# TensorE's order in the expert stretch of a two-layer diffusion step pinned to the program's, with the four column-tiled products of a value step kept together

## The chip, the cores and the metric

The kernel runs on one core of a Trainium2 chip. The metric is the device time of one execution in microseconds, the median of several runs. The engines are named as in the profile: PE (TensorE, the matmuls), PEld (its weight loads), DVE (VectorE), ACT (ScalarE), POOL (GpSimd, which also issues the gathers here) and SP (SyncE, which issues the plain loads).

## The reference, cut to what matters

One inference step of a backbone of two layers. Each layer mixes tokens (attention, a recurrent cell, pooling) and then adds an expert block. There are 128 prompt tokens and 256 latent tokens. The change touches the expert block alone:

```python
def peer_ffn(x, w_q, sub_keys, u_table, v_table):
    q = (xt @ w_q).reshape(T, PEER_HEADS, 2, PEER_HALF)
    s = jnp.einsum('thcd,hckd->thck', q, sub_keys).astype(F32)
    top_s, top_i = lax.top_k(s, PEER_TOPK)
...
    expert = i1 * PEER_N_KEYS + i2
    gate = jax.nn.softmax(best_s, axis=-1).astype(x.dtype)
...
        a = jax.nn.gelu(jnp.einsum('thkd,td->thk', u_table[eb], xb), approximate=False)
        return jnp.einsum('thk,thkd->td', gb * a, v_table[eb])
```

Every token chooses 128 of 16384 experts (8 heads of 16); each expert has a row in `u_table` and one in `v_table`, both of 1024 numbers.

## The kernel before

The latent tokens and the prompt tokens take different ways through the expert block, and both run at once in what is called the dense stretch below (function `dense`, one per layer).

*Latent tokens, dense.* All 16384 experts are computed for all 256 tokens, and a table of gates G, nearly all zeros, weighs the result. 64 iterations (`bp`) take 256 experts each. `up` loads two blocks of `u` and multiplies them with the tokens' activations into a bank A; `weigh` multiplies the activated result by G and splits it into a high and a low half, W; `down` loads two blocks of `v` and adds the products into four banks `po`. Each 32-bit product is made by `mm3` in three passes from high and low halves (high by high, low of one, low of the other): 48 up-products and 24 down-products an iteration. ScalarE casts the high halves (L105) and VectorE subtracts for the low ones (L106). The first 23 iterations' up-products (`LOOK`) are made ahead, unsplit (`whole`, L1087), while routing and the gate table G are built; iterations 23 to 63 are made inside the dense stretch.

*Prompt tokens, gathered.* The generator `experts` goes through 128 steps of scores (rows of `u` gathered by POOL, tiles `gu`, dot products on VectorE, L883) and then, once the dots are transposed (`dT`, L877, and copied as `wT`), through 64 value steps in a layer (L896). Value step s takes the gathered tiles 2s and 2s+1 (`gv`), each brought by two gathers of 256 KB on POOL's queue (L869), issued three tiles ahead into five buffers. It makes four products, q = 0 to 3, each with 32 columns of weights `wz` and so in its own strip of 32 columns of the array; each shows as two records, so a step has eight. `wz` has one buffer, refilled before steps 0, 16, 32 and 48: POOL clears it (L889), VectorE makes four small copies from `wT` (L893). The clearing stands in POOL's queue behind the gathers of tile 2s+4.

*What sets the order.* `dense` writes, for each iteration, `up`, `weigh`, `down`, then as many steps of `experts` as are due by then: in the first half of a layer's value steps one or two an iteration, later mostly one. A scheduler that simulates the program may then move an engine's instructions against one another as far as data allow. `tc.keep_in_program_order` (here `behind`) forbids that for one instruction: it stays behind everything that was written before it for the same engine. Before, only the first of the four products of a value step was so pinned.

Of the kernel before, what the change touches and what calls it, by code (L numbers as in the profile page):

```python
# [22 lines left out]
KC = 8  # L23
# [45 lines left out]
def tile_hybrid_step(ctx: ExitStack, tc: tile.TileContext, I, O):  # L69
# [29 lines left out]
        return t  # L99


    PASSES = ((0, 0), (0, 1), (1, 0))

    def split_into(hi, lo, src):
# [24 lines left out]
        split_into(hi, lo, raw)  # L129
        return hi, lo  # L130

    def mm3(out, a, b, first, last):
        for n, (x, y) in enumerate(PASSES):
            pe.matmul(out, a[x], b[y], start=first and n == 0, stop=last and n == 2, skip_group_check=True)  # L134

    class Room:

# [13 lines left out]
            return t  # L151

    GATH = Room(stay, row=("gath", NGATH), half="half", quarter="half")


    behind = tc.keep_in_program_order


    ident = ld("ident", [P, P], I["c_ident"], cst)
# [19 lines left out]
    def tsl(i):  # L179
        return slice(i * P, (i + 1) * P)  # L180
# [592 lines left out]
    class Prompt:  # L773
# [65 lines left out]
        def experts(self):  # L839
# [7 lines left out]
            for k in range(2 * P + LAG):  # L847
# [33 lines left out]
                if 0 <= j < P:  # L881
                    u = late.pop(j)
                    behind(ve.scalar_tensor_tensor(u, u, 1.0, self.h2n, op0=ALU.mult, op1=ALU.mult, accum_out=dots[:, j:j + 1]))  # L883
                elif j >= P and (j - P) % 2 == 1:
                    r, h = (j - P) // 4, (j - P) // 2 % 2
                    if r % 8 == 0 and h == 0:

                        wz = stay.tile([P, 8, 4, 32], F32, tag="row", bufs=1, name=f"wz{l}{r}")
                        gp.memset(wz, 0.0)  # L889
                        flat = wz.rearrange("p r j c -> p (r j c)")  # L890
                        for q in range(4):
                            at = 32 * q + r
                            ve.tensor_copy(flat[:, at:at + 7 * 129 + 1:129], wT[:, at:at + 8])  # L893
                    v = [late.pop(j - 1), late.pop(j)]
                    for q in range(4):
                        m = pe.matmul(self.acc[h][32 * q:32 * q + 32, :], wz[:, r % 8, q, :],  # L896
                                      v[q // 2][:, q % 2 * 512:q % 2 * 512 + 512], start=(r == 0), stop=(r == 31),
                                      skip_group_check=True)
                        if q == 0:
                            behind(m)  # L900
                yield

    def queries(l, most):
# [111 lines left out]
    class Experts:  # L1015
# [56 lines left out]
        def up(self, whole=None):  # L1072

            l, bp = self.l, self.next
            if bp == NP:
                return
            self.next += 1

            pa = bank("pv" if bp % 2 and self.pr.done < P + LAG else "A", f"A{l}{bp}")
            for j in range(2):  # L1080
                u = (load_split if whole is None else load_whole)(I["u_T"][l, 2 * bp + j], f"u{l}{bp}{j}")
                out = pa[:, j * 256:(j + 1) * 256]
                for k in range(KC):
                    if whole is None:
                        mm3(out, [t[:, tsl(k)] for t in u], [t[:, k, :] for t in self.hs], k == 0, k == KC - 1)
                    else:
                        pe.matmul(out, u[:, tsl(k)], whole[:, k, :], start=k == 0, stop=k == KC - 1, skip_group_check=True)  # L1087
            gl = self.lay.tile([P, 2, 2 * P], F32, tag="gl", bufs=LOOK[l] - 1, name=f"gl{l}{bp}")
            ac.activation(gl, pa.rearrange("p (j t) -> p j t", j=2), AF.Gelu)  # L1089
            self.acts[bp] = gl  # L1090
# [11 lines left out]
        def down(self, po, bp, w):  # L1102
# [6 lines left out]
            for i, j in ((0, 0), (0, 1), (1, 0), (1, 1)) if end else ((0, 0), (1, 0), (0, 1), (1, 1)):  # L1109
                for h in range(2):  # L1110
                    mm3(po[i][h], [t[:, j, tsl(i)] for t in w], [t[:, h * 512:(h + 1) * 512] for t in v[j]],
                        bp == 0 and j == 0, end and j == 1)

    def dense(l, ex, p3, po, pr):

# [228 lines left out]
```

## Time and profile before

| | us |
|---|---|
| median of 3 runs | 2739.42 (2739.12 to 2743.07) |
| the profiled execution, own time | 2746.87 |
| its span, first to last instruction | 2745.1 |
| PE busy in it | 2500.7 (91%) |
| DVE, ACT, POOL busy | 1722.4, 1045.5, 927.6 |
| mean granted TensorE clock | 0.944 of full speed |

The table gives the whole span. The dense stretches are where the change lies; they run from about 683 to 1388 us and from about 2042 to 2732 us. In a timeline a row gives the start, the duration, the engine with line and operation, the tile written and those read, and how many instructions were merged; in brackets stands the engine's idle time just before and what ended it.

### The profile page before, as it was taken

To read this page: it belongs to the slowest core of one execution; us is meant where nothing else is said; L and a number is where in the kernel's file an instruction comes from. 1 tells how busy PE (TensorE), PEld (TensorE's weight loads), DVE (VectorE), ACT (ScalarE), POOL (GpSimd) and SP (SyncE) were. 2 spreads that over 40 slices of the span, in tenths; PEclk is the share of its full clock that TensorE was granted. 3 is DMA by queue.
4 is the path that set the end of the run, shared out by engine and by line. 5 is a ranking of instruction groups with operands and counts; after the bars stand their busy time and mean duration, and the time that the engine had idled before them with its cause. 6 is when DMAs were issued, how large, how long until landed. Compare 5 with 4: busy or idle time off the path is not lost.

```text
span 2745.1 us, 37514 instructions
## 1 busy us (share of the span) xinstructions
PE 2500.7 (91%) x13834; PEld 1915.5 (70%) x13834; DVE 1722.4 (63%) x3768; ACT 1045.5 (38%) x1545; POOL 927.6 (34%) x794
## 2 busy tenths in 40 slices
PE   7998779896999999999989885979969999999998
PEld 3744568785988777765666464868859877777665
DVE  4555979866877444443565468798778844444446
ACT  3434411544434433332444352114444433343333
POOL 0000034101445666754400002231224556656541
PEclk9998989897999999999999878999979999999999
DMA  7485589678899889897835644886999988888985
GB/s 258 139 269 194 167 289 337 210 268 321 305 352 347 303 314 330 290 330 259 292 122 166 218 162 152 315 291 232 334 347 353 329 296 311 299 315 289 330 294 192
DMA packets 217547, 749.33 MB, mean 273 GB/s; under 512 B 28308, under 2 KB 30868, under 8 KB 215316
## 3 DMA queue, kind: packets, MB, share of 16 engines
q1 hardware_dynamic: 137236, 444.91, 46.8%
q0 software_dynamic: 77824, 268.48, 27.9%
q10 hardware_dynamic: 2304, 33.56, 3.1%
q8 instruction: 108, 1.77, 0.3%
q14 instruction: 75, 0.61, 0.1%
HBM read 706.99 MB, written 39.85 MB: 272 GB/s over the span
## 4 chain that ended last, share of the span: by engine, by line
PE 62%; DMA 13%; DVE 12%; issue 7%; POOL 3%; ACT 2%; SPq 0%; POOLq 0%; DVEq 0%; ACTq 0%
PE po L134 22%; PE A L134 13%; PE pv L896 6%; DMA gu<-in_peer_u,ei 4%; PE A L1087 4%; PE pj_i L134 4%; DMA v_r<-in_peer_v 3%; DVE gu L883 3%; DMA gv<-in_v_half,eiT 2%; DMA wm<-in_w_mod 2%; PE pm L305 2%; POOL gu L863 2%; PE pj_t L134 2%; POOL gv L869 2%; PE pj_o L134 1%
## 5 line engine op out<-in xcount | busy, mean ns | idle before, releaser
L869 POOL DMA_INDIRECT gv<-in_v_half,eiT x512 | 590.1, 1153 | 437.7 <-PE pv L896 288.4
L134 PE MATMUL po<-v_h,W 128*128 128x512 f32 x2048 | 668.8, 398 | 30.5 <-ACT W L105 16.0
L863 POOL DMA_INDIRECT gu<-in_peer_u,ei x256 | 324.5, 1267 | 1095.0 <-DVE gu L883 474.6
L134 PEld LDWEIGHTS po<-v_h,W 128*128 128x128 f32 x2048 | 388.8, 191 | 160.7 <-ACT W L105 44.1
L106 DVE TENSOR_TENSOR v_l<-v_r,v_h 128x1024 fp32r<-128x1024 f32 x256 | 313.0, 1224 | 273.7 <-ACT v_h L105 273.5
L134 PE MATMUL A<-hs,u_h 128*128 128x256 f32 x2624 | 482.7, 284 | 1.3 <-ACT u_h L105 0.9
L134 PEld LDWEIGHTS A<-hs,u_h 128*128 128x128 f32 x2624 | 406.8, 189 | 58.9 <-issue 34.4
L105 ACT CAST v_h<-v_r 128x1024 fp32r<-128x1024 f32 x256 | 268.4, 1049 | 385.7 <-PE po L134 155.4
L134 PE MATMUL po<-v_l,W 128*128 128x512 f32 x1024 | 406.0, 397 | 0.1
L134 PE MATMUL A<-hs,u_l 128*128 128x256 f32 x1312 | 370.7, 283 | 2.4 <-DVE u_l L106 2.4
L106 DVE TENSOR_TENSOR u_l<-u_r,u_h 128x1024 fp32r<-128x1024 f32 x164 | 199.1, 1224 | 275.3 <-ACT u_h L105 275.2
L883 DVE SCALAR_TENSOR_TENSOR gu<-gu,h2n 128x1024 f32<-128x1024 f32 x256 | 307.4, 1218 | 63.7 <-DMA gu<-in_peer_u,ei 63.1
L1087 PE MATMUL A<-hw,u_r 128*128 128x256 f32 x1472 | 339.1, 386 | 0.0
L1087 PEld LDWEIGHTS A<-hw,u_r 128*128 128x128 f32 x1472 | 276.5, 193 | 36.0
L105 ACT CAST u_h<-u_r 128x1024 fp32r<-128x1024 f32 x164 | 171.4, 1050 | 307.8 <-PE A L134 258.5
L134 PEld LDWEIGHTS A<-hs,u_l 128*128 128x128 f32 x1312 | 248.3, 189 | 10.9 <-issue 6.7
L134 PEld LDWEIGHTS po<-v_l,W 128*128 128x128 f32 x1024 | 195.6, 191 | 49.6 <-issue 11.7
L896 PE MATMUL pv<-gv,wz 128*32 128x512 f32 x1024 | 194.2, 605 | 5.9 <-DVE wz L893 3.1
L106 DVE TENSOR_TENSOR W<-gl,W 128x512 fp32r<-128x512 f32 x128 | 87.9, 688 | 52.0 <-ACT W L105 51.9
L105 ACT CAST W<-gl 128x512 fp32r<-128x512 f32 x128 | 79.0, 618 | 105.7 <-PE po L134 72.0
L1089 ACT ACTIVATE gl<-A 128x512 f32<-128x512 f32 x128 | 75.5, 595 | 110.9 <-DVE W L106 62.9
L1046 PE MATMUL G<-o,o 128*128 128x128 f16 x1024 | 89.9, 238 | 30.0 <-DVE o L1038 27.6
(424 smaller groups left out, 2982.0 us busy)
## 6 DMA issues: line engine op xcount, KB each, us to landing
u_r<-in_u_T SPq DMA_DIRECT2D x256, 512.0 KB, 5.9
v_r<-in_peer_v SPq DMA_DIRECT2D x256, 512.0 KB, 5.1
wm<-in_w_mod SPq DMA_DIRECT2D x96, 512.0 KB, 5.7
gates<-stage ACTq DMA_DIRECT2D x14, 2048.0 KB, 10.9
G<-gates SPq DMA_DIRECT2D x16, 1792.0 KB, 12.4
w_o_r<-in_w_out SPq DMA_DIRECT2D x32, 512.0 KB, 4.6
w_q_r<-in_w_q SPq DMA_DIRECT2D x32, 512.0 KB, 5.5
w_i_r<-in_w_in SPq DMA_DIRECT2D x24, 512.0 KB, 4.5
```

Of the source, the lines that this page charges most:

```text
L105: ac.copy(hi, src)
L106: ve.tensor_sub(lo, src, hi.bitcast(F32))
L134: pe.matmul(out, a[x], b[y], start=first and n == 0, stop=last and n == 2, skip_group_check=True)
L305: pe.matmul(pm[32 * j:32 * j + 32, :], silu[:, kc, :], w[:, jj * 512:(jj + 1) * 512], start=(kc == 0), stop=(kc == KC - 1), skip_group_che ...
L863: gp.indirect_dma_start(out=t, out_offset=None, in_=I["peer_u"], in_offset=bass.IndirectOffsetOnAxis(ap=ei[:, k:k + 1], axis=0))
L869: gp.indirect_dma_start(out=t[:, j * 512:(j + 1) * 512], out_offset=None, in_=I["v_half"], in_offset=bass.IndirectOffsetOnAxis(ap=eiT[:, h ...
L883: behind(ve.scalar_tensor_tensor(u, u, 1.0, self.h2n, op0=ALU.mult, op1=ALU.mult, accum_out=dots[:, j:j + 1]))
L896: m = pe.matmul(self.acc[h][32 * q:32 * q + 32, :], wz[:, r % 8, q, :], v[q // 2][:, q % 2 * 512:q % 2 * 512 + 512], start=(r == 0), stop= ...
L1046: m = pe.matmul(pg[:, tsl(t)], o2[:, z, :, t0 + t], o1[:, t0 + t, :], start=(z == 0), stop=(z == 1), skip_group_check=True)
L1087: pe.matmul(out, u[:, tsl(k)], whole[:, k, :], start=k == 0, stop=k == KC - 1, skip_group_check=True)
L1089: ac.activation(gl, pa.rearrange("p (j t) -> p j t", j=2), AF.Gelu)
```

## The change

Three kinds of products are pinned now. In `experts` all four products of a value step stay behind what was written before them, where only the first did. In `up`, inside the dense stretch (`whole is None`), the first pass of the first of the eight products of each half is pinned, and in `down` the first pass of every product. Nothing is added or left out, and no tile, buffer or transfer changes. The function `behind` is only defined earlier.

```diff
--- before.py
+++ after.py
@@ -99,6 +99,9 @@
         return t
 
 
+    behind = tc.keep_in_program_order
+
+
     PASSES = ((0, 0), (0, 1), (1, 0))
 
     def split_into(hi, lo, src):
@@ -129,9 +132,11 @@
         split_into(hi, lo, raw)
         return hi, lo
 
-    def mm3(out, a, b, first, last):
+    def mm3(out, a, b, first, last, pin=False):
         for n, (x, y) in enumerate(PASSES):
-            pe.matmul(out, a[x], b[y], start=first and n == 0, stop=last and n == 2, skip_group_check=True)
+            m = pe.matmul(out, a[x], b[y], start=first and n == 0, stop=last and n == 2, skip_group_check=True)
+            if pin and n == 0:
+                behind(m)
 
     class Room:
 
@@ -151,9 +156,6 @@
             return t
 
     GATH = Room(stay, row=("gath", NGATH), half="half", quarter="half")
-
-
-    behind = tc.keep_in_program_order
 
 
     ident = ld("ident", [P, P], I["c_ident"], cst)
@@ -896,8 +898,7 @@
                         m = pe.matmul(self.acc[h][32 * q:32 * q + 32, :], wz[:, r % 8, q, :],
                                       v[q // 2][:, q % 2 * 512:q % 2 * 512 + 512], start=(r == 0), stop=(r == 31),
                                       skip_group_check=True)
-                        if q == 0:
-                            behind(m)
+                        behind(m)
                 yield
 
     def queries(l, most):
@@ -1082,7 +1083,7 @@
                 out = pa[:, j * 256:(j + 1) * 256]
                 for k in range(KC):
                     if whole is None:
-                        mm3(out, [t[:, tsl(k)] for t in u], [t[:, k, :] for t in self.hs], k == 0, k == KC - 1)
+                        mm3(out, [t[:, tsl(k)] for t in u], [t[:, k, :] for t in self.hs], k == 0, k == KC - 1, k == 0)
                     else:
                         pe.matmul(out, u[:, tsl(k)], whole[:, k, :], start=k == 0, stop=k == KC - 1, skip_group_check=True)
             gl = self.lay.tile([P, 2, 2 * P], F32, tag="gl", bufs=LOOK[l] - 1, name=f"gl{l}{bp}")
@@ -1109,7 +1110,7 @@
             for i, j in ((0, 0), (0, 1), (1, 0), (1, 1)) if end else ((0, 0), (1, 0), (0, 1), (1, 1)):
                 for h in range(2):
                     mm3(po[i][h], [t[:, j, tsl(i)] for t in w], [t[:, h * 512:(h + 1) * 512] for t in v[j]],
-                        bp == 0 and j == 0, end and j == 1)
+                        bp == 0 and j == 0, end and j == 1, True)
 
     def dense(l, ex, p3, po, pr):
```

All TensorE instructions of the dense stretch now stand in the order in which the program writes them. The first place is value step 11 of the first layer, on PE. `pv01` is its bank, `gv022` and `gv023` its two gathered tiles, `po` a down-product of iteration 23, `A047` an up-product of iteration 47. Before:

```order
L134 MATMUL po011_5189<-v0231_l_7994,W0230_7981 128x512
L134 MATMUL po011_5189<-v0231_h_7993,W0231_7982 128x512
L896 MATMUL pv01_7283<-gv022_7900,wz00_7287 32x512 x2
L896 MATMUL pv01_7283<-gv023_7907,wz00_7287 32x512
L134 MATMUL A047_8034<-hs00_5176,u0470_h_8037 128x256
...
L134 MATMUL A047_8034<-hs01_5177,u0470_h_8037 128x256
L896 MATMUL pv01_7283<-gv023_7907,wz00_7287 32x512
L134 MATMUL A047_8034<-hs00_5176,u0470_l_8038 128x256
```

After:

```order
L137 MATMUL po011_5189<-v0231_l_7994,W0230_7981 128x512
L137 MATMUL po011_5189<-v0231_h_7993,W0231_7982 128x512
L898 MATMUL pv01_7283<-gv022_7900,wz00_7287 32x512 x2
L898 MATMUL pv01_7283<-gv023_7907,wz00_7287 32x512 x2
L137 MATMUL A047_8034<-hs00_5176,u0470_h_8037 128x256
```

The fourth product of the step stood eight up-products behind the other three, and now follows them. Over both layers the 128 steps stood in 146 unbroken runs: 62 of one product, 1 of two, 9 of three, 38 of four, 6 of six, 7 of seven and 23 of eight. Now there are 89: 50 of four and 39 of eight, that is one step and two steps. In the first layer steps 0, 11, 26 and 39 stand alone between up- and down-products and pairs begin at 1, 3, 5, 7, 9, 12 to 24 (even), 27 to 37 (odd), 40 and 42; in the second 0, 1, 6, 13, 18, 25, 30, 35, 42 stand alone and pairs begin at 2, 4, 7, 9, 11, 14, 16, 19, 21, 23, 26, 28, 31, 33, 36, 38, 40, 43 and 45. The steps behind these stand alone between down-products of one iteration, with two iterations' after steps 52 and 63 in the first layer, and after 47, 53 and 58 (and three after 63) in the second.

The second place is steps 31 and 32 of the first layer, on PE; step 31 is the last to use the weights `wz08` and step 32 the first to use `wz016`. Before (between the parts stand 48 up- and 19 down-products, then five more down-products):

```order
L134 MATMUL po011_5189<-v0341_h_9352,W0341_9341 128x512
L896 MATMUL pv01_7283<-gv062_9256,wz08_8392 32x512 x2
L896 MATMUL pv01_7283<-gv063_9263,wz08_8392 32x512 x2
L134 MATMUL A058_9403<-hs00_5176,u0580_h_9406 128x256
...
L134 MATMUL po010_5188<-v0351_h_9479,W0350_9467 128x512
L896 MATMUL pv00_7282<-gv064_9266,wz016_9393 32x512 x2
L896 MATMUL pv00_7282<-gv065_9273,wz016_9393 32x512 x2
L134 MATMUL po010_5188<-v0351_l_9480,W0350_9467 128x512
...
L134 MATMUL po011_5189<-v0351_h_9479,W0351_9468 128x512
L896 MATMUL pv01_7283<-gv066_9380,wz016_9393 32x512 x2
```

After:

```order
L137 MATMUL po011_5189<-v0341_h_9352,W0341_9341 128x512
L898 MATMUL pv01_7283<-gv062_9256,wz08_8392 32x512 x2
L898 MATMUL pv01_7283<-gv063_9263,wz08_8392 32x512 x2
L898 MATMUL pv00_7282<-gv064_9266,wz016_9393 32x512 x2
L898 MATMUL pv00_7282<-gv065_9273,wz016_9393 32x512 x2
L137 MATMUL A058_9403<-hs00_5176,u0580_h_9406 128x256
```

The two steps, which had a whole iteration's products between them, stand back to back. In the second layer they do so too. The order of POOL's queue is unchanged.

The third place is the start of the second layer's dense stretch, on PE. `G1314` is the last product of the gate table, `po1...` are down-products of iteration 0, `W100` its high and `W101` its low half, `A123` an up-product of iteration 23. Before:

```order
L1046 MATMUL G1314_16246<-o1131_16230,o2131_16232 128x128
L134 MATMUL po100_16273<-v100_h_16347,W100_16341 128x512
L134 MATMUL po100_16273<-v100_l_16348,W100_16341 128x512
L134 MATMUL po101_16274<-v100_h_16347,W100_16341 128x512
L134 MATMUL po101_16274<-v100_l_16348,W100_16341 128x512
...
L134 MATMUL po111_16276<-v100_h_16347,W100_16341 128x512
L134 MATMUL po111_16276<-v100_l_16348,W100_16341 128x512
L134 MATMUL po100_16273<-v100_h_16347,W101_16342 128x512
L134 MATMUL po101_16274<-v100_h_16347,W101_16342 128x512
```

After:

```order
L1047 MATMUL G1314_16246<-o1131_16230,o2131_16232 128x128
L137 MATMUL A123_16277<-hs10_16263,u1230_h_16280 128x256
...
L137 MATMUL A123_16277<-hs10_16263,u1231_l_16311 128x256
L137 MATMUL po100_16273<-v100_h_16347,W100_16341 128x512
L137 MATMUL po100_16273<-v100_l_16348,W100_16341 128x512
L137 MATMUL po100_16273<-v100_h_16347,W101_16342 128x512
L137 MATMUL po101_16274<-v100_h_16347,W100_16341 128x512
L137 MATMUL po101_16274<-v100_l_16348,W100_16341 128x512
```

The 48 up-products of iteration 23 now stand behind the gate table and ahead of the first down-product, and those of iteration 24 behind iteration 0's down-products, where both were mixed into the gate table's products; it is the same in the first layer. With them 7 to 8 us of VectorE's subtractions and dot products leave the stretch of the gate table. And the third pass, with the low half of W, follows each product's first two; before it stood behind eight products of the first two passes, in this iteration and in some 25 others ahead of `dT`.

## Rows read from the trace of the kernel before

**Rows 1.** The page's part on the chain of work that ended last: shares of the span by engine.

```profile
PE 62%; DMA 13%; DVE 12%; issue 7%; POOL 3%; ACT 2%; SPq 0%; POOLq 0%; DVEq 0%; ACTq 0%
```

**Rows 2.** Busy time by stretch: the stretch, its length, then busy time and instructions of PE, PEld, DVE, ACT and POOL, the granted clock, the DMA engines' busy share and GB/s. The first is late in the first layer's score steps, the second in its value steps.

```profile
785.00:853.00 68.00, 65.85 (x424) 59.77 (x423) 60.48 (x83) 30.97 (x36) 35.11 (x23) 1.00 0.96 361
...
917.00:972.00 55.00, 54.47 (x353) 42.24 (x352) 23.59 (x24) 19.30 (x22) 38.76 (x32) 1.00 0.92 328
```

**Rows 3.** The timeline of PE: five runs of the step products (L896), each with the row that follows it, and the start of a sixth.

```profile
917.70 1.92 PE L896 MATMUL pv<-gv,wz 128*32 128x512 f32 x16
919.55 0.50 PE L134 MATMUL A<-hs,u_h 128*128 128x256 f32 x2
...
930.89 2.75 PE L896 MATMUL pv<-gv,wz 128*32 128x512 f32 x16
933.58 0.51 PE L134 MATMUL A<-hs,u_h 128*128 128x256 f32 x2
...
1257.63 1.04 PE L896 MATMUL pv<-gv,wz 128*32 128x512 f32 x2
1258.60 0.73 PE L134 MATMUL po<-v_h,W 128*128 128x512 f32 x2
...
1309.19 1.06 PE L896 MATMUL pv<-gv,wz 128*32 128x512 f32 x8
1310.19 0.50 PE L134 MATMUL po<-v_h,W 128*128 128x512 f32 x1
...
1315.86 1.07 PE L896 MATMUL pv<-gv,wz 128*32 128x512 f32 x8
...
2512.99 1.92 PE L896 MATMUL pv<-gv,wz 128*32 128x512 f32 x14
...
2516.12 0.51 PE L134 MATMUL A<-hs,u_h 128*128 128x256 f32 x2
```

**Rows 4.** The instructions that write or read the tile pv: idle time of their engine just before them (us, times) and what ended it, then who waited for them.

```profile
  DMA gv<-in_v_half,eiT: 16.5, 30
  DVE wz L893: 7.3, 4
...
  POOL gv L869: 288.4, 96
```

**Rows 5.** The timeline of PE: the transposition of the dots, the first record of step 42 and the last down-product of the first layer; the same with step 45 in the second.

```profile
890.23 0.27 PE L877 MATMUL dT<-ident,dots 128*128 128x128 f32 x1
...
1208.98 1.48 PE L896 MATMUL pv<-gv,wz 128*32 128x512 f32 x10
...
1387.65 0.39 PE L134 MATMUL po<-v_h,W 128*128 128x512 f32 x1
...
2198.74 0.27 PE L877 MATMUL dT<-ident,dots 128*128 128x128 f32 x1
...
2567.40 1.91 PE L896 MATMUL pv<-gv,wz 128*32 128x512 f32 x12
...
2731.71 0.39 PE L134 MATMUL po<-v_h,W 128*128 128x512 f32 x1
```

**Rows 6.** The timelines of POOL and DVE in one period of the second layer: first the gather issues (the first, second, fourth and eighth, and the first of the next period), then two of VectorE's subtractions.

```profile
2271.14 1.91 POOL L869 DMA_INDIRECT gv<-in_v_half,eiT  x1 [6.56 <-PE pv L896]
2273.36 0.95 POOL L869 DMA_INDIRECT gv<-in_v_half,eiT  x1 [0.30 <-issue]
...
2275.86 1.94 POOL L869 DMA_INDIRECT gv<-in_v_half,eiT  x1 [0.30 <-issue]
...
2282.20 1.29 POOL L869 DMA_INDIRECT gv<-in_v_half,eiT  x1 [0.30 <-issue]
2284.34 1.91 POOL L869 DMA_INDIRECT gv<-in_v_half,eiT  x1 [0.84 <-PE pv L896]
...
2271.01 1.23 DVE L106 TENSOR_TENSOR v_l<-v_r,v_h 128x1024 fp32r<-128x1024 f32 x1 [0.92 <-ACT v_h L105]
2275.76 1.23 DVE L106 TENSOR_TENSOR u_l<-u_r,u_h 128x1024 fp32r<-128x1024 f32 x1 [3.52 <-ACT u_h L105]
```

**Rows 7.** The timelines of POOL, DVE and PE around the refill before step 32 of the first layer: the first gather and the clearing; the four copies; steps 31 and 32.

```profile
1125.79 1.91 POOL L869 DMA_INDIRECT gv<-in_v_half,eiT  x1 [0.84 <-PE pv L896]
...
1131.60 0.97 POOL L889 MEMSET wz<- 128x1024 f32 x1
...
1132.60 0.40 DVE L893 COPY wz<-wT 128x8 f32<-128x8 f32 x4 [1.82 <-POOL wz L889]
...
1124.43 1.06 PE L896 MATMUL pv<-gv,wz 128*32 128x512 f32 x8
...
1135.66 1.07 PE L896 MATMUL pv<-gv,wz 128*32 128x512 f32 x8
```

**Rows 8.** Step 48 of the first layer in the timeline of PE, and the stretch from it on in the view by stretches (columns as in rows 2).

```profile
1262.87 2.26 PE L896 MATMUL pv<-gv,wz 128*32 128x512 f32 x8 [3.08 <-DVE wz L893]
...
1262.40:1268.60 6.20, 5.73 (x16) 3.34 (x17) 2.51 (x8) 1.14 (x2) 2.86 (x3) 0.50 0.81 272
```

**Rows 9.** The timeline of PE: the first down-product of each layer.

```profile
682.97 0.79 PE L134 MATMUL po<-v_h,W 128*128 128x512 f32 x1 [13.24 <-ACT W L105]
...
2042.13 0.79 PE L134 MATMUL po<-v_h,W 128*128 128x512 f32 x1 [2.71 <-ACT W L105]
```

## The prediction

> **What bounds the kernel now.** I read the chain of waits first: TensorE holds 62% of it, DMA 13%, VectorE 12% [rows 1]. So time that TensorE loses in the two dense stretches comes back one for one, unless a transfer stands behind it. Next the timeline of TensorE there. In both value phases it goes from one matmul to the next almost without a gap (54.47 of 55.00 us busy in 917 to 972), but the DMA engines run beside it at 0.92 of their time and 328 GB/s, where the best stretch moved 361 [rows 2]. TensorE is the bound, DMA is close behind.
>
> Then the prices of the column-tiled products, as the time from a run's first product to the next other matmul [rows 3]. A lone product of a step takes 0.97 us (1257.63 to 1258.60), a whole quartet 1.00 (1309.19 to 1310.19), two steps back to back 1.85 (917.70 to 919.55). The price belongs to the run and not to its products: each splitting of a quartet costs one more 0.97.
>
> **Part 1, the quartets.** In the order of the kernel before the 128 steps stand in 146 runs: 110 of one to four products, 36 of six to eight. In the changed order there are 89: 50 single steps and 39 pairs of steps. By these prices the runs cost 110 x 1.00 + 36 x 1.85 = 176.6 us now, and 50 x 1.00 + 39 x 1.85 = 122.2 then: 54.4 saved, all on TensorE's path. The waits in front of them, on gathers 16.5 us and on refilled weights 7.3 [rows 4], change as well, so I make the sum from whole phases, by periods that the trace shows unbroken and free of waits. Up-products, down-products and a pair of steps: 917.70 to 930.89, 13.19 us; with a single step 13.19 - 0.85 = 12.34; at the end of a layer, down-products and a single step, 1309.19 to 1315.86, 6.67 [rows 3]. From a period, 24 down-products take 5.67.
>
> The phases now, from [rows 5]: first layer, transposed dots to step 42, 890.23 to 1208.98 = 318.8; from there to the last down-product's end (1387.65 + 0.39), 179.1; second layer, to step 45, 2198.74 to 2567.40 = 368.7; to the end, 164.7. Sum 1031.3. Both programs have the same matmuls between these points.
>
> In the new order: first layer, 4 single and 19 double periods, 49.4 + 250.6 = 300.0, and about 1.6 before step 0, since nothing may now slip in while its weights are made: 301.6. Its end: a pair and a down (7.5), 20 periods of 6.67 (133.4), two more downs (11.3): 152.2. Second layer: 9 single and 18 double, 111.1 + 237.4, and 3.2 for step 0: 351.7. Its end: 7.5 + 17 x 6.67 + 5 x 5.67 = 149.3. (The 1.6 and 3.2 are estimates: memset and copies of a refill take 1.4 in [rows 7].) Sum 954.8, so **76.5 us saved before new waits**. That is more than the 54.4, since waits of the kernel before are in its phases.
>
> **Part 2, waits that come in.** The instruction that waits is a pinned product on TensorE's own queue, and everything stands behind it: the next up- and down-products, and through them ScalarE's casts, the buffers, and SyncE's loads.
> - *Gathers.* A pair of steps needs 8 gather issues. From 2271.14 to 2283.49 they take 12.35 us, plus 0.84 until the next begins: as long as the period of 13.19 [rows 6]. Where paired runs follow each other, the second waits: 2.69 us in place of 1.85 at 930.89, 3.13 at 2512.99, the first and last of eight such runs (mean 1.3 more) [rows 3]. The next one, its gathers begun later, doesn't wait. So every second run of an unbroken series waits: by the lengths of the series (5, 7, 6, 2 pairs; then 2, 3, 2, 3, 2, 2, 3, 2) 15 beside the refills. 15 x 1.3 = 19.5.
> - *Refill at step 32.* Steps 31 and 32 stand in one pair in both layers, and step 32 needs new weights. Their memset stands in POOL's queue behind four gathers that wait for step 31's buffers. Now: step 31 at 1124.43, gathers from 1125.79, memset 1131.60, copies 1132.60 to 1133.00, and step 32 ran at 1135.66 behind up- and down-products that filled the time [rows 7]. Pinned, step 32 starts at the earliest some 8.8 us after step 31, that is 7.9 of pure wait. After a shorter wait at 1262.87 the granted clock was 0.50 in the stretch 1262.40 to 1268.60, the 1.2 GHz level, and half of 5.7 us was lost, 2.9 [rows 8]; I take 2.3. Together 10.2, twice: 20.4. Bounds: 7.9 each without the clock, 13 each if the gathers behind are late too.
> - *Smaller.* Step 16 is in front of a pair; its refill comes 14.6 us after the last use in the row of before, against a period of 13.19: 1.4, twice, 2.8. Step 48 of the first layer has only one down (6.67) against 8.8: 2.1 and some clock, 3.8 (in the second layer two downs cover it). 1.3 somewhere in the end phase. Sum 7.9.
>
> Together 47.8, leaving 28.7.
>
> **Part 3, the start of the dense stretches.** The up-products of iterations 23 and 24 leave the gate-table build and come behind it, with some 8 us of VectorE work; nothing else may fill TensorE there. In the first layer TensorE now waits 13.24 us for the first weights at 682.97 [rows 9]: iteration 23 fits into it, 24 adds 5.7 to the path, the build ends up to 8 earlier, and the stage behind runs at 0.96 of the DMA engines [rows 2], which gives an early start back. I take 0 (from 7 gained to 6 lost). In the second layer the wait is 2.71 [rows 9]: about 11.4 us come on the path (two times 48 up-products of 5.7, a period less down and pair), 7 of build go: 5 lost (1 to 9). Last, a down-product's first pass was pinned too. Before, in some 25 of the early downs eight products with the high half of W came ahead of the first that needs the low half; now two do. Six products of 0.236 us are 1.4 us of cover each, at most; W is late in few of them, and other waits there shrink: 3 lost (0 to 7). **Sum of part 3: 8 lost.**
>
> **The sum.** 76.5 - 47.8 - 8 = 20.7 us saved. The profiled execution's own time is 2746.87, its span 2745.1; it becomes 2726.2. It lies 7.45 above the median of 2739.42, so the median becomes 2718.7: **2719 us**, 0.8% faster.
>
> **Rivals.** A, *slower: the gathers set the period.* Place: POOL's queue in the 37 paired periods. An issue takes 0.95 us, but 1.91 and 1.94 where it begins beside VectorE's subtraction (2271.14 with 2271.01, 2275.86 with 2275.76) [rows 6]. Two of four subtractions per period do that now; with all four, the eight issues take 14.3 and with 0.84 behind them 15.1 us, against 13.19 + 0.65 that I count. Already a wait of 1.3 in all 37 in place of 15 adds 22 x 1.3 = 28.6: 2747. It decides from 0.94 us more in each of those 22. For it: 328 of 361 GB/s and POOL with no slack. Against: in the stretches of before every second run found its gathers landed.
> The Trainium skill, page "SBUF — State Buffer", section "SBUF: two separate sides", says that VectorE with two SBUF inputs and a GpSimd operation that reads SBUF lock the shared port pair against each other, and the second fully blocks. The 1.91 beside 0.95 agrees; by that rule alone every meeting costs a POOL issue up to a subtraction, which is what A prices with rows.
>
> B, *faster: the gathers keep up*, since after each wait POOL has a lead, and only the refills stay: 19.5 less, 2699; with the refill's clock loss gone as well 2695. For it: after single steps there is slack of four issues.
>
> C, *the clock falls at each gather wait.* 15 x 2.3 = 34.5 more: 2753. Against: the wait of 0.84 at 930.89 [rows 3] and what else lies in 917 to 972 left the granted clock at 1.00 [rows 2].
> The Trainium skill, page "TensorE: Matmul & The Clock Gate", section "HAM oscillation — how this bites in real kernels", tells that waits on transfers between bursts put the clock back each time; that row speaks against it for short waits, and [rows 8] for it after the long one.
>
> D, *it doesn't do what it says*: the order shows no run that isn't four or eight products, so only a price could fail: 2739.
>
> **How the numbers follow.** Forecast 0.55; waits half again as large as counted, which ends near no change, 0.10; A 0.15; B 0.15; C 0.03; D 0.02. About 0.2% (5.5 us) is what can be told from no change. Faster 0.55 + 0.15 = 0.70; same 0.12; slower 0.18. The range reaches from B's 2695 to just short of A's 2747: 2695 to 2745.
>
> **What would show it.** Runs of eight and sixteen records of the step product only, 50 and 39 of them, at 1.00 and 1.85 apart from waits. At each pair (31, 32) one wait of 7 to 9 us on VectorE's weight copies, and half clock after it. Gather waits about 1.3, in every second run: in every run, A; in none, B. The end phases some 27 and 15 us shorter before waits, the middle phases a few us longer with them. The first up-products of the dense stretch of the second layer some 5 us later after the gate table. Wrong would be above all the count of gather waits, then the refill's price.

## The result, and the profile after

The changed kernel takes 2699.94 us (median of 4 runs, 2694.92 to 2715.15) against 2739.27 of the kernel before (4 runs, 2737.71 to 2743.07): ratio 0.9864, 95% interval 0.9821 to 0.9906. That is some 37 to 39 us saved, where 20.7 were forecast; the time lies in the range of 2695 to 2745, near its lower end. The profiled execution took 2703.24 us, its span is 2701.5 (before: 2746.87 and 2745.1).

First the forecast's phases. The timeline of PE of the changed kernel, at the same six points as [rows 5]:

```profile
884.05 0.28 PE L879 MATMUL dT<-ident,dots 128*128 128x128 f32 x1
...
1202.23 1.07 PE L898 MATMUL pv<-gv,wz 128*32 128x512 f32 x8
...
1360.77 0.39 PE L137 MATMUL po<-v_h,W 128*128 128x512 f32 x1
...
2164.31 0.27 PE L879 MATMUL dT<-ident,dots 128*128 128x128 f32 x1
...
2535.76 1.48 PE L898 MATMUL pv<-gv,wz 128*32 128x512 f32 x10
...
2688.11 0.39 PE L137 MATMUL po<-v_h,W 128*128 128x512 f32 x1
```

The differences of these starts (the last ones with the 0.39 us of the row) give the phases. A second profile of either program stands beside, from two experiments below whose instructions stand in the same order: quartet_pins_only is the program of before, dense_pins_only that of the change.

| phase, us | before | its program again | forecast, with waits | after | its program again |
|---|---|---|---|---|---|
| first layer, dots to step 42 | 318.8 | 318.4 | 323.6 | 318.2 | 319.0 |
| to the last down-product | 179.1 | 178.1 | 157.3 | 158.9 | 158.3 |
| second layer, dots to step 45 | 368.7 | 369.7 | 372.4 | 371.5 | 368.9 |
| to the last down-product | 164.7 | 164.7 | 149.3 | 152.7 | 151.6 |
| sum: the dense stretches from the dots on | 1031.2 | 1031.0 | 1002.6 | 1001.3 | 997.8 |

The sums repeat within 0.2 and 3.5 us. So the dense stretches saved 29.9 and 33.2 us, where 28.7 were forecast: at the ends of the layers, as the forecast has it, and next to nothing in the middle. Of these sums the runs of value products themselves, each from its first product to the next other matmul and with the waits inside it, took 186.1 and 186.7 us in the two profiles of before's program and 166.0 and 161.7 in those of the change. The rest of the dense stretches took 845.1 and 844.3, and then 835.3 and 836.1. So 20.1 and 25.0 us of the gain lie in the runs.

The runs and their prices, in the timeline of PE of the changed kernel (rows as in [rows 3]):

```profile
910.79 1.92 PE L898 MATMUL pv<-gv,wz 128*32 128x512 f32 x14
913.00 1.04 PE L898 MATMUL pv<-gv,wz 128*32 128x512 f32 x2 [0.29 <-DMA gv<-in_v_half,eiT]
913.98 0.50 PE L137 MATMUL A<-hs,u_h 128*128 128x256 f32 x2
...
925.26 1.92 PE L898 MATMUL pv<-gv,wz 128*32 128x512 f32 x16
927.12 0.50 PE L137 MATMUL A<-hs,u_h 128*128 128x256 f32 x2
...
1213.42 1.06 PE L898 MATMUL pv<-gv,wz 128*32 128x512 f32 x8
1214.42 0.50 PE L137 MATMUL po<-v_h,W 128*128 128x512 f32 x1
...
1220.09 1.07 PE L898 MATMUL pv<-gv,wz 128*32 128x512 f32 x8
```

A quartet takes 1.00 us again (1213.42 to 1214.42), a pair of steps 1.86 (925.26 to 927.12), the end period 6.67 (1213.42 to 1220.09). The pair at 910.79 took 3.19, that is 1.34 of wait for a gather, and the next one, at 925.26, none: every second run of a series.

The view of the instructions that write or read the tile pv, as in [rows 4]: what they waited for, and who waited for them.

```profile
  DVE wz L895: 44.8, 13
  DMA gv<-in_v_half,eiT: 33.5, 32
...
  POOL gv L871: 257.6, 88
```

Both waits grew, gathers from 16.5 to 33.5 us and weights from 7.3 to 44.8. (Weight loads and matmuls can both book a wait, so the sums are above the time that was lost.)

The refill at step 32 of the first layer, in the timelines of PE, POOL and DVE, which answers to [rows 7]:

```profile
1114.00 1.06 PE L898 MATMUL pv<-gv,wz 128*32 128x512 f32 x8
1122.26 2.24 PE L898 MATMUL pv<-gv,wz 128*32 128x512 f32 x8 [7.19 <-DVE wz L895]
1124.43 0.80 PE L137 MATMUL A<-hs,u_h 128*128 128x256 f32 x2
...
1115.37 1.91 POOL L871 DMA_INDIRECT gv<-in_v_half,eiT  x1 [2.47 <-PE pv L898]
...
1121.03 0.97 POOL L891 MEMSET wz<- 128x1024 f32 x1
...
1122.03 0.39 DVE L895 COPY wz<-wT 128x8 f32<-128x8 f32 x4 [5.58 <-POOL wz L891]
```

Step 31 starts at 1114.00 and step 32 at 1122.26, 8.26 later, where 8.8 were forecast. Four gathers stand on POOL ahead of the clearing, as expected. Step 32 itself took 2.17 us (to 1124.43) in place of 1.00. The view by stretches (columns as in [rows 2]) shows the clock beside it, and beside a stretch with gather waits alone:

```profile
897.00:966.00 69.00, 67.86 (x441) 52.94 (x441) 29.60 (x30) 24.52 (x28) 48.57 (x40) 1.00 0.89 308
...
1114.00:1124.00 10.00, 2.81 (x17) 0.66 (x16) 1.93 (x6) 1.54 (x2) 5.72 (x5) 0.72 0.79 267
1124.00:1128.20 4.20, 4.20 (x32) 3.77 (x29) 0.00 (x0) 0.36 (x1) 2.85 (x3) 0.85 0.31 81
1128.20:1136.00 7.80, 7.80 (x46) 6.73 (x44) 4.40 (x5) 3.31 (x4) 0.95 (x1) 1.00 0.70 224
```

After the wait of 7 us the granted clock is low for about 3 us and then back at 1.00, the 2.4 GHz level. In 897 to 966, with waits of 1.3 and 1.9 us on gathers, it stays at 1.00. The other refill, in the second layer, cost the same: the pair took 8.65 us more than its price, this one 8.57, against 10.2 forecast with the clock behind it.

The start of the first layer's dense stretch, in the timeline of PE, answers to [rows 9]:

```profile
666.82 0.50 PE L137 MATMUL po<-v_h,W 128*128 128x512 f32 x1 [1.54 <-ACT W L108]
...
668.76 1.22 PE L137 MATMUL po<-v_h,W 128*128 128x512 f32 x2 [1.21 <-DVE W L109]
```

The wait of 13.24 us is gone but for 1.54: the up-products of iteration 23 fill it, and the gate table ends earlier. Behind it stands a wait of 1.21 for the low half of W, which the forecast had put at 1.4 at most. From the first gate product to the transposed dots the first layer took 379.6 and 377.8 us in the two profiles of before's program, and 376.6 and 375.9 in the two of after's; the second layer 325.5 and 326.5, and 330.6 and 324.9. Together that is 2.1 us lost in the one pair of profiles and 3.5 gained in the other, where 8 lost were forecast.

The rest of the gain lies where the change edits nothing: 12.6 us in one pair and 4.4 in the other from the first layer's last down-product to the second layer's first gate product (485.2 and 481.2 us in before's program, 472.6 and 476.8 in after's), and 3.2 and 1.8 ahead of the first layer's first gate product, where both programs have the same order on TensorE. The stretch between the layers was planned anew in places, on VectorE and GpSimd above all.

### The profile page after: what moved, and what is told of

Same layout as the page of the kernel before. It is cut to its first block, busy times and chain, and to the rows that moved or that the text cites. A ratio compares the mean times of both kernels' runs of the same rounds, so it can differ in the third digit from the quotient of the medians.

```text
span 2701.5 us, 37514 instructions
## 1 busy us (share of the span) xinstructions
PE 2442.7 (90%) x13834; PEld 1913.5 (71%) x13834; DVE 1721.7 (64%) x3768; ACT 1048.9 (39%) x1545; POOL 941.7 (35%) x794
## 5 line engine op out<-in xcount | busy, mean ns | idle before, releaser
L865 POOL DMA_INDIRECT gu<-in_peer_u,ei x256 | 334.9, 1308 | 1071.6 <-DVE gu L885 466.3
L898 PE MATMUL pv<-gv,wz 128*32 128x512 f32 x1024 | 148.4, 608 | 29.8 <-DVE wz L895 20.4
L1047 PEld LDWEIGHTS <-o 128*128 128x128 f16 x1024 | 84.6, 150 | 49.1 <-DVE o L1039 39.0
L257 PE MATMUL pj_q<-hw,w_q_r 128*128 128x256 f32 x512 | 116.6, 390 | 0.0
```

The costliest lines, as they stand in the source:

```text
L257: pe.matmul(pj[:, 0:n], w[:, tsl(k)], rhs(k), start=k == 0, stop=k == KC - 1, skip_group_check=True)
L865: gp.indirect_dma_start(out=t, out_offset=None, in_=I["peer_u"], in_offset=bass.IndirectOffsetOnAxis(ap=ei[:, k:k + 1], axis=0))
L1047: m = pe.matmul(pg[:, tsl(t)], o2[:, z, :, t0 + t], o1[:, t0 + t, :], start=(z == 0), stop=(z == 1), skip_group_check=True)
```

## The experiments

A name of a kernel is that of its run. "Dense sum" is the sum of the four phases above. Each ratio is to the kernel before on the same chip.

### Fewer gathers, or smaller ones

half_gathers fetches one half row of a value tile in place of two. The other half is left out, and the third and fourth product read the first half again:

```diff
-                        for j in range(2):
+                        for j in range(1):
...
-                                       v[q // 2][:, q % 2 * 512:q % 2 * 512 + 512], ...
+                                       v[q // 2][:, 0:512], ...
```

> The changed kernel with one gather for each value tile in place of two (256 KB, four issues for a pair of steps); the other half of a tile is not fetched, and the third and fourth product read the first half again, so part of the value rows is left out. In the profile of the changed kernel the runs of value products exceed their prices by 50.1 us: 17.2 at the two step-32 refills, 3.6 at the two steps 0, 4.8 at steps 16 and 48, and so 24.5 on gathers. Theory (POOL's issue pace makes the gather waits): gather waits under 3 us, refill waits about 6 each since two gathers fewer stand ahead of the clearing; 25 to 30 us faster than the changed kernel's 2700, about 2672. Rival (the DMA engines' rate makes them): the same here; the next kernel tells the two apart. Second rival (gather waits don't set the end, another transfer comes late in their place): under 10 us faster.

Measured: 2672.12 us, ratio 0.9764 (0.9722 to 0.9806), dense sum 968.0. The view of pv, idle before its instructions:

```profile
  DVE wz L895: 30.9, 8
  PE po L137: 2.6, 1
```

No wait on a gather is left at all, and the two step-32 refills cost 6.0 and 5.9 us over the price, as expected with two gathers fewer ahead of the clearing. So the waits on gathers do lengthen the whole time.

half_bytes keeps both gathers and halves each, so that it too leaves half of the values out:

```diff
-  ...indirect_dma_start(out=t[:, j * 512:(j + 1) * 512], ..., in_=I["v_half"],
+  ...indirect_dma_start(out=t[:, j * 512:j * 512 + 256], ..., in_=I["v_half"].rearrange("n (a b) -> (n a) b", b=256),
...
-  v[q // 2][:, q % 2 * 512:q % 2 * 512 + 512]
+  v[q // 2][:, q % 2 * 512:q % 2 * 512 + 256].unsqueeze(1).to_broadcast([P, 2, 256])
```

> The changed kernel with both gathers of a tile kept, each of half the bytes (256 numbers a row, 128 KB); the products read these 256 columns twice, and the rows come from another part of the table, so values are left out. Same number of issues on POOL, half the gathered bytes. Theory (POOL's issue pace): an issue still takes 0.95 to 1.9 us, gather waits stay near 18 to 25 us and the time within 10 us of the changed kernel, 2690 to 2700. Rival (the rate of the DMA engines): gather waits under 5 us, 20 us or more faster, about 2675.

Measured: 2707.45 us, ratio 0.9862 (0.9824 to 0.9901), dense sum 991.7. The view of pv:

```profile
  DVE wz L895: 49.3, 16
  DMA gv<-in_v_half,eiT: 7.6, 16
```

Neither expectation held whole. The gather waits fell from 33.5 to 7.6 us, which the theory of POOL's pace doesn't have. The time is the changed kernel's, as that theory has it, but this can't be read for it: in this profile VectorE waits 13.0 us in the second layer's gate table for a reason that is told below with refill_apart, and that hides what the dense stretches gained. Both bytes and issues count. Half the bytes took some 8 us from the dense sum (999.5 on the mean of two profiles to 991.7), and half the issues at the same bytes another 24 (991.7 to 968.0), of which some 5 are the shorter refills. By what the runs took above their prices, apart from those at a refill, bytes weigh more: 24.5 and 21.1 us in the two profiles of the changed program, 8.9 in half_bytes, none in half_gathers. Which weighs more is not shown. Nor is it shown that the issue itself is what half_gathers saves, since it halves the number of fetched rows as well.

### The refill at step 32, cured in two ways

clear_dve clears the weights on VectorE:

```diff
-                        gp.memset(wz, 0.0)
+                        ve.memset(wz, 0.0)
```

> The changed kernel with the clearing of the step weights on VectorE in place of POOL, so that it no longer stands behind four gathers. Theory: the wait at step 32, 8.6 us in each layer, falls to 2.5 us or less (a clearing of about 1 us and copies of 0.4 behind what VectorE has in hand), no half clock after it, the waits at steps 16 and 48 go: 17 to 22 us faster than the changed kernel, about 2680. Rival (the wait at step 32 is held by something else too, such as gathered tiles that come late, and moves there): 6 us or less.

Measured: 2703.40 us, ratio 0.9853 (0.9811 to 0.9895), dense sum 990.2. The two pairs (31, 32) took 3.4 and 3.0 us more than their price, no longer 8.6. That is a little more than the 2.5 expected, and the whole time is not the expected 17 to 22 us shorter than the changed kernel's 2699.94.

refill_apart moves the order of steps, so that step 31 stands alone:

```diff
+            stop = want
+            if pr.done >= P + LAG + 2:
+                stop = min(want, pr.done + 4)
+                if pr.done < P + LAG + 64 < stop:
+                    stop = P + LAG + 64
-            while pr.done < want:
+            while pr.done < stop:
                 next(pr.others)
```

> The changed kernel with the order of value steps shifted so that step 31 stands alone and step 32 opens a pair one iteration later (48 up- and 24 down-products between them, about 11 us, against the 8.8 that a refill needs); the number of runs stays 50 and 39. Theory: no wait at step 32 in either layer and no half clock behind it, the rest as in the changed kernel: 17 to 22 us faster, about 2680. Rival (the stall is only moved: the gathers behind the clearing come late for the next pair): 8 us or less.

Measured: 2707.94 us, ratio 0.9875 (0.9836 to 0.9914), dense sum 984.7. The view of pv:

```profile
  DMA gv<-in_v_half,eiT: 33.4, 37
  DVE wz L895: 13.5, 8
```

The waits on weights fell from 44.8 to 13.5 us and those on gathers stayed. So in the dense stretches the cure did what it should, 9 and 15 us against the mean of 999.5, and yet neither kernel was measurably faster than the changed one. Most of where that went is in the profile of refill_apart, second layer, gate table; the timelines of PE and DVE:

```profile
1926.93 8.42 PE L1088 MATMUL A<-hw,u_r 128*128 128x256 f32 x38
1935.19 0.38 PE L1008 MATMUL st<-ident,ix 128*128 128x128 f32 x2
...
1936.34 1.29 DVE L1037 TENSOR_TENSOR o<-iotaT,tab 128x1024 f16<-128x1024 f16 x2 [14.26 <-ACT tab L1010]
```

The three transposes of the second half's routing result (`st`) stand behind 38 up-products made ahead, and VectorE, whose one-hot products the gate table is made of, waits 14.26 us once. clear_dve has that wait with 12.9 us. In the changed kernel the transposes lie between the up-products, and the waits at that place are 6.2 and 1.1 us. Nothing in this code was edited: the scheduler plans the whole program anew, and a change in the first layer gave it another plan in the second. From the first gate product to iteration 25's up-products the second layer took 191.2 us in refill_apart and 193.4 in clear_dve, and 183.5 and 180.5 in the two profiles of the changed program. In refill_apart the first layer lost some 6 us too, from its first gate product to the dots (382.3 against 376.6 and 375.9); what did that is not shown.

### Which pins do it

dense_pins_only takes the pins on the second to fourth value product back and keeps those on up- and down-products:

```diff
-                        behind(m)
+                        if q == 0:
+                            behind(m)
```

> The changed kernel with the pins on up- and down-products kept and those on the second to fourth value product taken back. Its instructions stand on every engine in the same order as in the changed kernel, 50 runs of four and 39 of eight. Theory (the pins on the neighbours group the quartets, those on the quartets themselves do nothing): the same time, 2690 to 2710, ratio to before 0.982 to 0.991; and a second profile of the same program tells which of the differences outside the dense stretches repeat: those of the order (the dot products in the second layer's routing) do, those of the clock in the mixing of the second layer (8.5 us) need not. Rival (a pin costs or brings something of its own beside the order): outside these bounds.

Measured: 2708.13 us, ratio 0.9869 (0.9835 to 0.9904), dense sum 997.8.

quartet_pins_only is the other half:

```diff
-            if pin and n == 0:
+            if False and pin and n == 0:
```

> The change with its pins on all four value products alone, and none on up- and down-products. The order on every engine is that of the kernel before, 146 runs. Theory: no difference from before, ratio 0.996 to 1.004, and the runs of value products cost as before. Rival (the title's part of the change brings the gain): 0.986. Its profile is a second look at the program of before: the low clock in the mixing of the second layer may or may not come back.

Measured: 2742.15 us, ratio 0.9991 (0.9965 to 1.0016), dense sum 1031.0.

So the whole gain comes from the pins on the up- and down-products. Without them the instructions of every engine stand as in the kernel before, in 146 runs; with them alone they stand as in the changed kernel. A pin keeps an instruction behind what was written ahead of it; it doesn't keep later ones from slipping in between. That the third and fourth product are pinned holds nobody off. That the next up- or down-product is pinned behind them does. What the up-products' pins and the down-products' each bring was not told apart.

The two are second profiles as well, and show how much an unchanged program varies. Up to the first gate product of the first layer the program of before took 510.7 and 519.8 us, that of the change 507.5 and 518.0. In the second layer's mixing, up to its first query product, the changed program is 6.2 us shorter in the one pair of profiles (336.6 to 330.4) and 4.2 longer in the other (328.3 to 332.5). The largest piece of this is one stretch in which TensorE's order is the same in all four profiles. Its first matmuls in the timeline of PE and the view by stretches, of the kernel before, and then of the changed one at the same place:

```profile
1520.11 1.05 PE L305 MATMUL pm<-wm,silu 128*32 128x512 f32 x4 [1.73 <-DMA wm<-in_w_mod]
1521.09 1.95 PE L692 MATMUL oT<-PT,nat 128*64 128x256 f32 x4
...
1520.00:1536.00 16.00, 15.89 (x64) 6.33 (x64) 3.46 (x13) 2.22 (x8) 0.00 (x0) 0.68 0.57 194
```

```profile
1490.51 1.05 PE L307 MATMUL pm<-wm,silu 128*32 128x512 f32 x4
1491.49 1.08 PE L694 MATMUL oT<-PT,nat 128*64 128x256 f32 x4
...
1490.50:1502.00 11.50, 11.50 (x65) 4.84 (x64) 3.89 (x14) 2.33 (x8) 0.00 (x0) 1.00 0.88 297
```

Nearly the same matmuls stand in both, at a granted clock of 0.68 after a wait of 1.73 us, and at 1.00 without one. In the other pair it is the other way round: the changed program waited 1.54 us there and its clock fell (0.66 in 1500.6 to 1515.8 of dense_pins_only), the program of before waited 0.75 and kept 1.00 (1523.8 to 1534.4 of quartet_pins_only). The same matmuls took 15.2 us at the low clock and 10.6 without it. So this is not the order's doing.

### The start of the dense stretch

start_free leaves the up-products of iterations 23 and 24 unpinned:

```diff
-  ..., k == 0, k == KC - 1, k == 0)
+  ..., k == 0, k == KC - 1, k == 0 and bp >= LOOK[l] + 2)
```

> The changed kernel without pins on the up-products of iterations 23 and 24, so that they mix into the gate table's products again as in the kernel before; the rest stays pinned. The changed kernel's profile has the first up-product of iteration 25 5.4 us sooner after the first gate product in the first layer than before and 1.4 later in the second, and 2.5 and 3.7 us more from there to the transposed dots. Theory (these ups belong to both): the first layer loses some 3 to 5, the second gains some 2 to 5, in all within 5 us of the changed kernel. Rival (the start is a main part of the gain): 10 us or more slower than the changed kernel.

Measured: 2718.79 us, ratio 0.9907 (0.9874 to 0.9940), dense sum 1003.1, 10.7 us slower than dense_pins_only on the same chip. The rival was right that the start matters: from the first gate product to the dots the first layer takes 382.8 us, 6.5 more than the mean of the changed program's two profiles, and the second 338.5, 10.7 more. The second layer has a wait of 14.2 us on the transposes' casts, the same as above, so only the first layer's 6.5, from one profile, can be put down to the unpinned start.

### Both cures, and the transposes set free

> The changed kernel with both cures: step 31 alone and step 32 an iteration later, and the step weights cleared on VectorE. Each of them took 11 and 17 us from the two dense stretches (from the transposed dots to the last down-product: 1001.3 us in the changed kernel, 990.2 and 984.7), but the whole times, 2703 and 2708, show no gain. Theory (the gain is there and is hidden by differences of 10 to 20 us from execution to execution in the other stretches): dense stretches near 980 us, and in five rounds beside the changed kernel's own program some 15 us less than it. Rival (a shorter dense stretch is given back elsewhere): no difference from it of over 5 us.

apart_dve joins two diffs from above:

```diff
-                        gp.memset(wz, 0.0)
+                        ve.memset(wz, 0.0)
...
+                if pr.done < P + LAG + 64 < stop:
+                    stop = P + LAG + 64
```

Measured: 2711.50 us, ratio 0.9876 (0.9836 to 0.9916), dense sum 988.1, and the wait on the casts behind the transposes 19.7 us. The rival held: against the changed kernel's own program on the same chip (2708.13) nothing was gained. In its profile the stretch between the layers is longer as well, 488.0 us against 472.6 and 476.8, so the gate table is not the whole of what hides the cures.

apart_st is refill_apart without the pin on these transposes:

```diff
-            behind(pe.transpose(pt[:, 0:P], src, ident))
+            pe.transpose(pt[:, 0:P], src, ident)
```

> The kernel with steps 31 and 32 apart, and in addition without the pin on the three transposes that bring the routing result of each latent half into the gate tables. In the four kernels with a changed plan (steps apart, clearing on VectorE, both, ups of 23 and 24 free) VectorE waited 12.9 to 19.7 us once in the second layer's gate table for the casts behind these transposes, which stood behind 38 up-products made ahead; in the kernel before that wait was 0.8 in three, in the changed kernel none of the longest. In this order 22 stand there. Theory (the cure of the dense stretch is real, about 15 us, and that wait hides it): the wait falls to 6 to 9 us, from the first gate product to the first up-product of iteration 25 in the second layer some 185 us in place of 191, the dense stretches near 985, the ratio to before 0.978 to 0.985. Rival (gains in the dense stretch are given back in any case): 0.986 to 0.990.

Measured: 2700.95 us, ratio 0.9834 (0.9803 to 0.9865), dense sum 983.8. The wait is 10.4 us and not 6 to 9, the stretch in the second layer 189.5 and not 185; the ratio lies where the theory had it.

dve_st is clear_dve with the same edit:

```diff
-                        gp.memset(wz, 0.0)
+                        ve.memset(wz, 0.0)
...
-            behind(pe.transpose(pt[:, 0:P], src, ident))
+            pe.transpose(pt[:, 0:P], src, ident)
```

> The kernel with the step weights cleared on VectorE, and in addition without the pin on the transposes of the routing result. Theory as for the one before: the wait of 12.9 us in the second layer's gate table falls to 6 to 9, the dense stretches stay near 990, ratio to before 0.979 to 0.986. Rival: 0.986 to 0.990.

Measured: 2695.26 us, ratio 0.9843 (0.9807 to 0.9880), dense sum 991.6, the wait 9.3 us. Over the kernels this wait grows with the number of up-products that stand just ahead of the second half's transposes: 7.4 us with 18 (half_gathers), 9.3 and 10.4 with 22 (dve_st, apart_st), 12.9 to 14.3 with 38 (clear_dve, half_bytes, start_free, refill_apart), 19.7 with 64 (apart_dve).

apart_st and dve_st have the lowest ratios of the kernels that compute everything. Their intervals overlap with the changed kernel's 0.9864, so that they beat the kernel before is measured, and that they beat the changed one is not.

## Why the prediction came out as it did

- **Prices and periods: right.** 1.00 and 1.85 us and the periods held; the saving before new waits, 76.5 in the forecast, came out at 73.7 and 72.7 (the 29.9 and 33.2 saved, with the 43.8 and 39.5 that the runs then took above their prices). The order did put the 128 steps into 89 runs.
- **Gathers: right in kind.** In the changed kernel's profile every second run of a series waits, at 910.79 by 1.34 us; in its program's second profile nearly so (the run at step 20 waits and the one at step 7 doesn't). Over both layers the gather waits came to 24.5 and 21.1 us over the prices in the two profiles, against 19.5 and 1.3 forecast. Rival A needed them in every run; they weren't, and the clock did not fall behind them (rival C). The forecast named POOL's issue pace as the cause; half_bytes shows that the bytes have a share.
- **The refill at step 32: right in place and mechanism, a little too dear.** 8.57 and 8.65 us, with a short stretch of low clock in them, against 10.2. That the dense sum came within 1.2 to 4.5 us of the forecast is in part luck: dearer gathers are made up by these refills and by the ones at steps 16 and 48 (4.6 and 4.4 us against 6.6). The Trainium skill, page "TensorE: Matmul & The Clock Gate", section "HAM oscillation — how this bites in real kernels", tells of a kernel whose waits on transfers between bursts put the clock back each time; the wait of 7.19 us agrees with it, and the gather waits of 1.3 and 1.9 us, shorter than the waits of its example, left the clock at 1.00.
- **The term that failed is part 3, "Sum of part 3: 8 lost".** It was mis-sized: 2.1 lost and 3.5 gained in two pairs of profiles. The forecast took 0 for the first layer from a range of 7 gained to 6 lost; between gate table and dots it gained 3.0 and 1.9, since the wait of 13.24 us was filled, and start_free puts the pinned start at 6.5. In the second layer it took 5 lost; 5.1 were lost in the one pair of profiles and 1.6 gained in the other. That term rests on the wait of 2.71 before the first down-product, and this wait is not a fixed one: in the second profile of before's program it is 10.48. The sign named for it, iteration 25's up-products 5 us later after the gate table's first product, came as 1.4 later in the one pair and 4.9 sooner in the other. How much the 3 us for the low halves of W was off is not told apart.
- **What no term had: the stretch between the layers,** 4.4 to 12.6 us shorter. The mixing in it gained 6.2 in one pair and lost 4.2 in the other, mostly by the clock, which the order doesn't explain. The remainder, in the routing, is shorter in both pairs (6.4 and 8.6): TensorE waits there for the first half's routing result from VectorE, 16.85 and 22.21 us in before's program and 11.47 and 14.27 in the change's. Whether that is the change's own (a new plan for VectorE) or chance stays open: half_bytes, which keeps the pins, has 16.80.

Put together, by the profiles, whose spans are 43.6 and 42.8 us apart (the medians 39): 29.9 and 33.2 us from the dense stretches against 28.7; part 3 with 2.1 lost and 3.5 gained against 8 lost; 12.6 and 4.4 between the layers and 3.2 and 1.8 ahead of the first gate product, for which the forecast had nothing. So the forecast's 20.7 was about half of the gain, by part 3 and by stretches of which much varies from execution to execution. What the text ahead of the forecast doesn't tell apart is whose pins matter: it lists those on the third and fourth product with the others, and the pins on the quartets themselves change nothing.

## What to carry to other kernels

Count runs, not products: where a kind of matmul costs about a microsecond for each unbroken run, whether the run holds one product or four, pinning the neighbours so that nothing can slip in saves it, and the pin belongs on the instruction that would slip in. Before you pin, look for the place where a strict order sets two instructions side by side between which a refill has to happen; it costs the whole refill, here 8.6 us twice. And where a scheduler plans the whole program, judge a cure by its own stretch in two profiles as well as by the total: a plan that changes in the other layer can take 10 us back.

## What the runs showed that was not expected

An unchanged order takes times that differ by 10 us up to the first gate product alone (507.5 and 518.0 us). What makes that difference there is not shown. In the second layer's mixing one cause of such differences is visible: one stretch of some 60 matmuls has a low granted clock in two of four profiles, with waits of 1.73 and 1.54 us just ahead of it, and 1.00 in the other two, with a wait of 0.75 or none. In the dense stretch waits of 1.3 to 1.9 us left the clock at 1.00.
